# Differential attention: the transposes of a step written in front of the next projection, and the value matmuls written as all high parts, then all low parts

## The chip, the cores and the metric

The kernel runs on one core of one Trainium2 chip. The metric is device time in microseconds (us) of one execution; 1 us is about 0.06% of the whole. Engines are named as in the profile: PE (TensorE matmuls) with PEld (its weight loads), DVE (VectorE), ACT (ScalarE), POOL (GpSimd) and SP (SyncE, which only issues transfers here).

## What is computed

The program is one decoder block: an RMS norm and one wide input projection, two attention mixers side by side, a gated merge, an output projection and a SwiGLU network. The change touches mixer A, differential attention, with 4 heads, blocks of 128 queries and 1024 positions:

```python
def one_block(i):
    s0 = i * DIFF_Q_BLOCK
    qb = lax.dynamic_slice_in_dim(q, s0, DIFF_Q_BLOCK, axis=1)
    s = jnp.einsum('bqhcd,bkhcd->bhcqk', qb, k).astype(jnp.float32) * scale
    qpos = s0 + jnp.arange(DIFF_Q_BLOCK)
    causal = kpos[None, :] <= qpos[:, None]
    p = jax.nn.softmax(jnp.where(causal, s, NEG_INF), axis=-1)
    a = p[:, :, 0] - lam * p[:, :, 1]
    return jnp.einsum('bhqk,bkhe->bqhe', a.astype(v.dtype), v)
```

Each head has two score matrices (c = 0 and 1); the second softmax is subtracted from the first with the weight lam, and the difference multiplies the values.

## The kernel before

Every float32 product is made of fp32r matmuls: an operand is split into a high part (a rounded copy, made by ACT or DVE) and a low part (the rest, made by DVE), and the products high x high, high x low and low x high are added up in PSUM. In the value product the two parts of v lie side by side, so that one matmul of 256 columns (line 497, the **high** value matmul) gives high x (high, low), and one of 128 columns (line 498, the **low** value matmul) adds low x high.

Mixer A is a loop of 32 **steps**, n = 8h + i for head h and query block i (lines 541 to 561). Before the change, iteration n of the loop writes down, in this order: `d_project(n+2)`, the **projection** of a later step, 24 matmuls of 384 columns into PSUM bank b1 (lines 159 to 161), then the rope products (lines 288 to 290) and the split of v (lines 420, 421), which read the bank and free it; `d_transpose(n+1)`, four **query transposes** (lines 436, 437) into bank b0, from where ACT makes qh (line 442), DVE ql (443) and ACT the transposed keys kT (444); `d_scores(n+1)`, the **scores** of a step (lines 461 to 464) and their softmax (minimum on DVE, line 465; exponential on ACT, 466; lines 468 to 471); `d_values(n)`, which for up to four key blocks at a time makes **probability transposes** (line 486), also into bank b0, then ah on ACT (491) and al on DVE (492), and then the value matmuls into bank b2; and one or two **merge units**, each 24 matmuls of 512 columns into bank b3 (`merge_unit`, lines 315 to 338), work of another part of the program that is put here to fill TensorE.

A step has i + 1 key blocks, so for i of 4 and more there are two groups of probability transposes, the first of four blocks, the second of one to four. Both groups and the query transposes share bank b0: each has to wait until ACT and DVE have read the one before.

This written order is not the order of the engines. A scheduler in the tile framework takes it as a priority, plays the program on a model of time and gives each engine a fixed list of instructions; each engine then runs its list in order. So what the change does to an engine's list is seen in the lists themselves, not in the diff.

The projections and merge units are the work that stands on TensorE's list between a transpose and the matmul that needs its result. It is called **cover** below.

Of the kernel before, what the change touches and what calls it, by code (L numbers as in the profile page):

```python
# [94 lines left out]
def hybrid_block(ctx: ExitStack, tc: tile.TileContext, x, positions, attn_norm_g, w_in, diff_lambda,  # L95
# [3 lines left out]
    V, A, G, T = nc.vector, nc.scalar, nc.gpsimd, nc.tensor  # L99
# [137 lines left out]
    def bank(i):  # L237
        return psum.tile([128, 512], F32, name="b%d" % i, bufs=1)

    def tr_tile():  # L240
        banks, n = turn["tr"]
        turn["tr"] = (banks, n + 1)
        return bank(banks[n % len(banks)]).rearrange("p (a b) -> p a b", b=128)
# [58 lines left out]
    def flat(ap):  # L302
        return ap.rearrange("p a b -> p (a b)")
# [9 lines left out]
    st, mg_done = {}, [0]  # L313
# [92 lines left out]
    with pool("da", bufs=2) as da, pool("das", bufs=2) as das:  # L406
# [24 lines left out]
        def d_transpose(n):  # L431
            h, i = divmod(n, NT)
            qd, ks = st.pop(("qk", n))
            tp = tr_tile()
            for c in range(2):
                T.transpose(tp[:, c], flat(qd[:, c]), ident)
                ins = T.transpose(tp[:, 2 + c], flat(ks[:, c]), ident)
            if GT and n >= DH * NT - GT:
                st["last"] = ins
            qh = da.tile([128, 2, 128], R, name="qh")  # L440
            ql = da.tile([128, 2, 128], R, name="ql")
            A.activation(qh, tp[:, 0:2], AF.Copy)
            V.tensor_sub(ql, tp[:, 0:2], qh)
            A.activation(st["kT", h][:, :, i * 128:(i + 1) * 128], tp[:, 2:4], AF.Copy)
            st["q", n] = (qh, ql)
# [28 lines left out]
        def d_values(n):  # L474
            h, i = divmod(n, NT)
            p0 = st.pop(("p", n))
            if i == 0:
                st["y", h] = (da.tile([128, NT, 128], F32, name="yraw"), das.tile([128, NT], F32, name="yss"))
            yraw, yss = st["y", h]
            o = bank(2)[:, :256]  # L480
            parts = []
            for b0 in range(0, i + 1, 4):
                nb = min(4, i + 1 - b0)
                tp = tr_tile()
                for b in range(nb):
                    ins = T.transpose(tp[:, b], p0[:, (b0 + b) * 128:(b0 + b + 1) * 128], ident)
                if b0 == 0 and n >= DH * NT - GLN:
                    st["last"] = ins
                ah = da.tile([128, 4, 128], R, name="ah")
                al = da.tile([128, 4, 128], R, name="al")  # L490
                A.activation(ah[:, :nb], tp[:, :nb], AF.Copy)
                V.tensor_sub(al[:, :nb], tp[:, :nb], ah[:, :nb])
                parts.append((b0, nb, ah, al))
            for b0, nb, ah, al in parts:
                for b in range(nb):
                    vb = flat(st["vv", h][:, b0 + b])
                    T.matmul(o, ah[:, b], vb, start=(b0 + b == 0), stop=False)
                    T.matmul(o[:, 0:128], al[:, b], vb[:, 0:128], start=False, stop=(b0 + b == i))
            ot = da.tile([128, 128], F32, name="ot")
            A.activation(ot, o[:, 128:256], AF.Copy)  # L500
            V.tensor_add(yraw[:, i], o[:, 0:128], ot)
            A.activation(ot, yraw[:, i], AF.Square, accum_out=yss[:, i:i + 1])
# [9 lines left out]
        def compressed_mask():  # L512
            cm32 = da.tile([128, 2, HD], F32, name="cm32", bufs=1)
            for tb in range(0, NT, 2):
                G.memset(cm32, 0.0)
                G.affine_select(cm32, cm32, pattern=[[128, 2], [-16, HD]], compare_op=OP.is_ge, fill=BIG,
                                base=tb * 128 - 31, channel_multiplier=1)
                G.tensor_copy(cmask[:, tb:tb + 2], cm32)
# [13 lines left out]
        N = DH * NT  # L532
# [6 lines left out]
            return first + int(sum(cw[:n + 1]) / sum(cw) * (2 * (2 * KD + NQX) - RES - first) + RES * max(0, n + 1 - N + RLN) / RLN + 1e-6)  # L539

        for n in range(-2, N):
            if n + 2 < N:
                d_project(n + 2)
            if n == -2:
                lam_scalar()
            if n == 10:
                compressed_mask()
            if 0 <= n + 1 < N:
                d_transpose(n + 1)
            if SF and 0 <= n + 1 < N:  # L550
                d_scores(n + 1)
            if n >= 0:
                d_values(n)
            if not SF and 0 <= n + 1 < N:
                d_scores(n + 1)
            while mg_done[0] < mg_target(n):
                merge_unit(mg_done[0])
                mg_done[0] += 1
            if n >= 0:
                if n >= NT and n % NT == 0:  # L560
                    d_norm(n // NT - 1)
# [268 lines left out]
    with lined("na", bufs=2) as na:  # L830
# [137 lines left out]
        for n, u in enumerate(units):  # L968
# [3 lines left out]
            i, hp, br = u  # L972
# [33 lines left out]
    with lined("br") as br, pool("brp", space=PSUM) as bp:  # L1006
# [25 lines left out]
        for n in range(2 * KD):  # L1032
            b, dm = divmod(n, KD)
# [390 lines left out]
    for n in range(NS):  # L1424
        i, p = divmod(n, HF)
# [54 lines left out]
```

## Time and profile before

| | us |
|---|---|
| median of 3 runs (1718.57 to 1719.31) | 1718.66 |
| the profiled execution, its own time | 1721.26 |
| its span in the trace | 1719.3 |
| TensorE busy in the span | 1647.1 |
| mixer A's steps in the trace | about 45 to 485 |

The page of the profile gives busy time per engine and 40 slices over the span. The timeline gives each instruction with its start, its duration and, in square brackets, the idle time before it and who ended it. Matmuls overlap in their records: the duration of one includes a tail of about 0.2 us that the next one hides, so what a matmul costs is read from start to start.

### The profile page before, as it was taken

The numbers are of one execution on the slowest core, as the hardware profiler recorded it, in microseconds if no ns is written. First come the engines' busy times: TensorE is split into PE (matmuls) and PEld (weight loads), VectorE is DVE, ScalarE is ACT, GpSimd is POOL, SyncE is SP. The second block draws the span as 40 slices with busy tenths as digits, with TensorE's granted clock in tenths as the row PEclk, the third lists the DMA queues.
The fourth block names the chain that finished last, engine by engine and source line by source line (L and its number), as shares of the span: only waits on it lengthen the run. The fifth ranks groups of instructions, "written<-read, shape, count | busy, mean of one in ns | idle before, by whom it ended". The sixth has DMA issues, their size and how long they took to land.

```text
span 1719.3 us, 25072 instructions
## 1 busy us (share of the span) xinstructions
PE 1647.1 (96%) x9025; PEld 1423.3 (83%) x9025; DVE 1090.3 (63%) x2156; ACT 775.1 (45%) x1652; POOL 441.5 (26%) x626
## 2 busy tenths in 40 slices
PE   4999999999999999999999997999999999999997
PEld 3988888988889998998878885788888888888886
DVE  8554545546348768888855339565656556686667
ACT  3334333434424247878854234433333333344445
POOL 4532322323222336657625210011100101000000
PEclk8999999999999999999999998999999999999999
DMA  6120211113213000100184421333332332674433
GB/s 209 47 80 25 81 43 44 50 44 95 86 59 99 29 28 15 50 17 17 26 285 159 172 86 50 111 116 117 113 108 92 102 113 97 209 246 120 135 96 140
DMA packets 150635, 163.68 MB, mean 95 GB/s; under 512 B 11616, under 2 KB 114048, under 8 KB 150512
## 3 DMA queue, kind: packets, MB, share of 16 engines
q1 hardware_dynamic: 138272, 124.90, 23.3%
q0 software_dynamic: 9760, 31.94, 4.9%
q10 hardware_dynamic: 2480, 5.25, 1.0%
q8 instruction: 71, 1.16, 0.3%
q14 instruction: 52, 0.43, 0.1%
HBM read 117.76 MB, written 44.30 MB: 94 GB/s over the span
## 4 chain that ended last, share of the span: by engine, by line
PE 82%; DVE 7%; issue 5%; ACT 3%; POOL 2%; DMA 1%; SPq 0%; ACTq 0%; POOLq 0%; DVEq 0%
PE mm L1140 8%; PE mm L1141 8%; PE mm L1142 8%; PE b L159 5%; PE b L160 5%; PE b L161 5%; PE s L874 3%; PE b L927 3%; PE mm L1386 3%; PE mm L1385 3%; PE mm L1387 3%; PE b L938 3%; PE s L159 2%; PE s L161 2%; PE s L160 2%
## 5 line engine op out<-in xcount | busy, mean ns | idle before, releaser
L1133 ACT ACTIVATE oh<-S 128x512 fp32r<-128x512 f32 x88 | 55.7, 633 | 142.2 <-PE mm L1141 140.1
L159 PE MATMUL b<-uh,mg_h 128*128 128x512 f32 x288 | 114.8, 399 | 0.7 <-ACT mg_st L337 0.7
L160 PE MATMUL b<-ul,mg_h 128*128 128x512 f32 x288 | 113.7, 395 | 0.0
L161 PE MATMUL b<-uh,mg_l 128*128 128x512 f32 x288 | 112.9, 392 | 0.0
L874 PE MATMUL s<-kN,qN 128*128 128x320 f32 (+5 forms) x384 | 100.8, 365 | 3.7 <-ACT p L891 2.7
L942 DVE TENSOR_TENSOR pl<-b,ph 128x512 fp32r<-128x512 f32 (+1 forms) x152 | 90.5, 613 | 12.8 <-ACT ph L941 11.8
L941 ACT ACTIVATE ph<-b 128x512 fp32r<-128x512 f32 (+1 forms) x152 | 80.2, 544 | 32.2 <-PE b L938 30.9
L161 PE MATMUL b<-pw_h,ul 128*128 128x384 f32 x256 | 89.1, 348 | 4.9 <-DVE ul L219 4.9
L891 ACT ACTIVATE p<-s,mn 128x640 f32<-128x640 f32 (+7 forms) x128 | 89.2, 703 | 7.7 <-DVE mn L885 2.4
L159 PE MATMUL b<-pw_h,uh 128*128 128x384 f32 x256 | 90.2, 352 | 2.0 <-ACT uh L218 1.4
L160 PE MATMUL b<-pw_l,uh 128*128 128x384 f32 x256 | 88.7, 347 | 3.5 <-DVE pw_l L269 3.5
L1133 ACT ACTIVATE oh<-raw 128x512 fp32r<-128x512 f32 x66 | 41.5, 632 | 108.3 <-PE mm L1141 105.9
L898 POOL TENSOR_TENSOR p<-p,sm 128x640 f32<-128x640 f32 (+3 forms) x64 | 89.1, 1414 | 2.5
L1387 PE MATMUL mm<-oh,ol 128*128 128x512 f32 x218 | 84.8, 389 | 0.0
L1386 PE MATMUL mm<-ol,oh 128*128 128x512 f32 x218 | 84.8, 389 | 0.0
L938 PE MATMUL b<-ident,p 128*128 128x128 f32 x528 | 83.0, 275 | 1.6 <-POOL p L895 1.0
L465 DVE TENSOR_REDUCE mn<-s 128x1 f32<-128x128 f32 (+7 forms) x64 | 46.0, 753 | 53.9 <-PE s L464 53.8
L1134 DVE TENSOR_TENSOR ol<-S,oh 128x512 fp32r<-128x512 f32 x88 | 59.6, 686 | 31.0 <-ACT oh L1133 26.7
L159 PE MATMUL s<-pw_h,uh 128*128 128x256 f32 (+1 forms) x256 | 75.8, 296 | 2.6 <-ACT xs L648 1.6
L927 PE MATMUL b<-ph,vN 128*128 128x256 f32 x264 | 75.1, 302 | 0.0
L160 PE MATMUL s<-pw_l,uh 128*128 128x256 f32 (+1 forms) x256 | 74.3, 290 | 0.0
L161 PE MATMUL s<-pw_h,ul 128*128 128x256 f32 (+1 forms) x256 | 74.0, 289 | 0.0
(451 smaller groups left out, 5146.8 us busy)
## 6 DMA issues: line engine op xcount, KB each, us to landing
raw<-in_w_gate_dram SPq DMA_DIRECT2D x22, 512.0 KB, 5.1
raw<-in_w_up_dram SPq DMA_DIRECT2D x22, 512.0 KB, 4.6
mg_raw<-in_w_in_dram SPq DMA_DIRECT2D x18, 512.0 KB, 4.6
mgd<-mg_st POOLq DMA_DIRECT2D x32, 256.0 KB, 3.7
sg<-mgd SPq DMA_DIRECT2D x16, 512.0 KB, 4.6
pw_raw<-in_w_in_dram SPq DMA_DIRECT2D x24, 256.0 KB, 3.8
b<-in_w_down_dram SPq DMA_DIRECT2D x22, 256.0 KB, 5.9
xt<-in_x_dram SPq DMA_DIRECT2D x8, 512.0 KB, 5.1
```

The costliest lines, as they stand in the source:

```text
L159: T.matmul(ps, ah, bh, start=(i == 0), stop=False)
L160: T.matmul(ps, ah, bl, start=False, stop=False)
L161: last = T.matmul(ps, al, bh, start=False, stop=(i == n - 1))
L874: T.matmul(s_[:, c], qN[:, 2 * hp + es[c * len(es) // 2], i * 128:(i + 1) * 128], kNs[br][:, v, g, c0:c0 + cw], start=(v == 0), stop=(v == 1))
L927: T.matmul(o, lhsT, rhs, start=(done == 0), stop=(done == total - 1))
L938: T.transpose(tp[:, 2 * (b - b0) + e], p[:, e, b * 128:(b + 1) * 128], ident)
L1133: A.activation(wh, src, AF.Copy)
L1140: T.matmul(ps, w[0][:, k], b[0][:, k], start=(first and k == 0), stop=False, **kw)
L1141: T.matmul(ps, w[0][:, k], b[1][:, k], start=False, stop=False, **kw)
L1142: T.matmul(ps, w[1][:, k], b[0][:, k], start=False, stop=(k == 3), **kw)
L1386: T.matmul(ps, ah[:, ts], wl, start=False, stop=False, **kw)
L1387: T.matmul(ps, al[:, ts], wh, start=False, stop=(p == HF - 1), **kw)
```

## The change

Two pieces of mixer A are written in another order. In the loop, `d_transpose(n+1)` stands in front of `d_project(n+2)`. In `d_values`, the loop over the key blocks is split in two: first every high value matmul of the step, then every low one. The matmuls, their shapes and their number stay the same; the low one's moving operand is named in another way but is the same columns. Lines behind the edit are 3 higher in the changed kernel (the low matmul's is 501 instead of 498, yraw's 504 instead of 501).

```diff
@@ -495,7 +495,10 @@
                 for b in range(nb):
                     vb = flat(st["vv", h][:, b0 + b])
                     T.matmul(o, ah[:, b], vb, start=(b0 + b == 0), stop=False)
-                    T.matmul(o[:, 0:128], al[:, b], vb[:, 0:128], start=False, stop=(b0 + b == i))
+            for b0, nb, ah, al in parts:
+                for b in range(nb):
+                    vh = st["vv", h][:, b0 + b, 0]
+                    T.matmul(o[:, 0:128], al[:, b], vh, start=False, stop=(b0 + b == i))
@@ -539,14 +542,14 @@
         for n in range(-2, N):
+            if 0 <= n + 1 < N:
+                d_transpose(n + 1)
             if n + 2 < N:
                 d_project(n + 2)
...
-            if 0 <= n + 1 < N:
-                d_transpose(n + 1)
             if SF and 0 <= n + 1 < N:
```

The engines' lists show what the scheduler makes of it. Up to step 0 nothing moves and behind mixer A next to nothing; SP's list has one load of merge weights six places earlier. Within mixer A the query transposes keep their place behind the last low matmul of a step in both lists; it is the projections and merge units that change places with the rest. Three places are shown; a name like b_3450 is one tile, here one use of a bank.

**Place 1: PE's list, values of step 21 (i = 5), second group.** b_3450 are the step's sums, b_3460 is the second group of probability transposes, b_3964 a projection. Before:

```order
L497 MATMUL b_3450<-vv,ah 128x256
L159 MATMUL b_3964<-pw_h,uh 128x384
L160 MATMUL b_3964<-pw_l,uh 128x384
L161 MATMUL b_3964<-pw_h,ul 128x384
L486 MATMUL b_3460<-ident,p_3291 128x128 x2
L498 MATMUL b_3450<-vv,al 128x128
L497 MATMUL b_3450<-vv,ah 128x256
L498 MATMUL b_3450<-vv,al 128x128
```

In the changed kernel the two transposes into b_3460 stand 20 merge matmuls ahead of these rows (b_4050 is the merge unit's bank):

```order
L159 MATMUL b_4050<-uh,mg_h 128x512
L160 MATMUL b_4050<-ul,mg_h 128x512
L161 MATMUL b_4050<-uh,mg_l 128x512
L497 MATMUL b_3450<-vv,ah 128x256 x2
L501 MATMUL b_3450<-vv,al 128x128 x6
L436 MATMUL b_3511<-ident,qd 128x128
L437 MATMUL b_3511<-ident,ks 128x128
L436 MATMUL b_3511<-ident,qd 128x128
```

Before, the second group is followed at once by the low matmul of an earlier block and then by alternating pairs; now most of a merge unit stands between the transposes of the second group and their high matmuls, and the low matmuls come last.

**Place 2: PE's list, scores of step 9 (head 1, block 1).** b_1696 and b_1695 are the probability transposes and the sums of step 8. Before, the last query transposes of step 9 and what follows them:

```order
L436 MATMUL b_1663<-ident,qd 128x128
L437 MATMUL b_1663<-ident,ks 128x128
L159 MATMUL b_1714<-uh,mg_h 128x512
L160 MATMUL b_1714<-ul,mg_h 128x512
L161 MATMUL b_1714<-uh,mg_l 128x512
```

And, still before, the end of the scores of step 9 and what follows them:

```order
L463 MATMUL s<-causalb,identb 128x128
L464 MATMUL s<-kT,ql 128x256
L486 MATMUL b_1696<-ident,p_1539 128x128
L159 MATMUL b_2151<-pw_h,uh 128x384
L160 MATMUL b_2151<-pw_l,uh 128x384
L161 MATMUL b_2151<-pw_h,ul 128x384
```

In the changed kernel, from the last query transposes of step 9 to the high matmul of step 8:

```order
L436 MATMUL b_1623<-ident,qd 128x128
L437 MATMUL b_1623<-ident,ks 128x128
L461 MATMUL s<-kT,qh 128x256
L463 LDWEIGHTS identb
L463 MATMUL s<-causalb,identb 128x128
L464 MATMUL s<-kT,ql 128x256
L461 MATMUL s<-kT,qh 128x256
L463 LDWEIGHTS identb
L463 MATMUL s<-causalb,identb 128x128
L464 MATMUL s<-kT,ql 128x256
L486 MATMUL b_1696<-ident,p_1539 128x128
L497 MATMUL b_1695<-vv,ah 128x256
```

Before, a whole merge unit stands between the query transposes and the scores, and 22 matmuls of a projection between the probability transpose and its high matmul (the first rows of each are shown); now there is nothing in either gap. Over the whole list, the gap between query transposes and scores is empty in 6 steps before (8 and 27 to 31) and in 8 now (9, 16, 23, 25 and 28 to 31); in 6 more it now holds two merge matmuls (17, 22), three (15), or three matmuls of a projection (24, 26, 27). The gap between a group of probability transposes and its first high matmul held seven matmuls or more before; now it is empty at steps 8, 16 and 24 (one block) and for the first group of step 22 (four blocks), and holds one matmul for the second groups of steps 23 (four blocks) and 28 (one). Two merge units that had two transposes and seven value matmuls between them at step 29 now have the two transposes alone.

**Place 3: DVE's list and PE's, around the scores of step 23 (i = 7).** b_3612 and b_3621 are the first and second group of probability transposes of step 22, which come right behind these scores; b_3611 are its sums. DVE before:

```order
L288 TENSOR_TENSOR t_3989<-b_3964,ropeC 128x256
L289 TENSOR_TENSOR t_3990<-b_3964,ropeS 128x4x32
L290 TENSOR_TENSOR t_3990<-b_3964,ropeS 128x4x32
L421 TENSOR_TENSOR vv<-b_3964,vv 128x128
L465 TENSOR_REDUCE mn<-s 128x1 x2
L492 TENSOR_TENSOR al<-b_3612,ah 128x512
```

DVE now:

```order
L465 TENSOR_REDUCE mn<-s 128x1 x2
L288 TENSOR_TENSOR t_3999<-b_3974,ropeC 128x256
L289 TENSOR_TENSOR t_4000<-b_3974,ropeS 128x4x32
L290 TENSOR_TENSOR t_4000<-b_3974,ropeS 128x4x32
L492 TENSOR_TENSOR al<-b_3612,ah 128x512
L468 RECIPROCAL rc<-sm 128x2
```

PE now, from the end of these scores:

```order
L463 MATMUL s<-causalb,identb 128x128
L464 MATMUL s<-kT,ql 128x512
L486 MATMUL b_3612<-ident,p_3429 128x128 x4
L497 MATMUL b_3611<-vv,ah 128x256 x4
L486 MATMUL b_3621<-ident,p_3429 128x128 x3
L159 MATMUL b_4088<-pw_h,uh 128x384
```

Before, the rope reads and the split of v stand ahead of the two minima (line 465), and on PE a projection separates the first group from the second; now the rope reads stand between the minima and al (line 492), and PE has the second group's transposes four high matmuls behind the first group's.

## Rows read from the trace of the kernel before

**Rows 1.** The page, busy time of TensorE and its share of the span

```profile
PE 1647.1 (96%) x9025; PEld 1423.3 (83%) x9025; DVE 1090.3 (63%) x2156; ACT 775.1 (45%) x1652; POOL 441.5 (26%) x626
```

**Rows 2.** Waits, 40 to 490 us: who waited for whom, total us, times, longest

```profile
PEld b L498 <- DVE al L492: 4.3, 9, 0.7
```

**Rows 3.** Timeline of PE in step 14: start, duration, instruction, idle before, releaser

```profile
265.94 0.38 PE L497 MATMUL b<-vv,ah 128*128 128x256 f32 x1
266.80 0.33 PE L498 MATMUL b<-vv,al 128*128 128x128 f32 x1 [0.48 <-DVE al L492]
266.96 0.33 PE L497 MATMUL b<-vv,ah 128*128 128x256 f32 x1
267.13 0.22 PE L498 MATMUL b<-vv,al 128*128 128x128 f32 x1
267.19 0.33 PE L497 MATMUL b<-vv,ah 128*128 128x256 f32 x1
```

**Rows 4.** Timeline of PE in mixer B: sixteen 64-column matmuls in a row

```profile
670.27 2.06 PE L841 MATMUL s<-kC,qN 128*128 128x64 f32 x16
```

**Rows 5.** Timeline, query transposes to scores with no cover (blocks 3 and 4)

```profile
409.75 0.27 PE L437 MATMUL b<-ident,ks 128*128 128x128 f32 x1
410.48 0.42 DVE L443 TENSOR_TENSOR ql<-b,qh 128x256 fp32r<-128x256 f32 x1 [0.27 <-ACT qh L442]
411.37 0.50 PE L461 MATMUL s<-kT,qh 128*128 128x512 f32 x1 [1.35 <-ACT kT L444]
...
419.48 0.27 PE L437 MATMUL b<-ident,ks 128*128 128x128 f32 x1
420.23 0.73 PE L461 MATMUL s<-kT,qh 128*128 128x512 f32 x2 [0.47 <-ACT qh L442]
```

**Rows 6.** Timeline, probability transposes to ah and al, one block and four

```profile
236.62 0.27 PE L486 MATMUL b<-ident,p 128*128 128x128 f32 x1
237.24 0.29 DVE L492 TENSOR_TENSOR al<-b,ah 128x128 fp32r<-128x128 f32 x1
...
383.73 0.60 PE L486 MATMUL b<-ident,p 128*128 128x128 f32 x4
384.36 0.60 ACT L491 ACTIVATE ah<-b 128x512 fp32r<-128x512 f32 x1 [2.85 <-PE b L486]
```

**Rows 7.** Timeline, scores of 1024 columns: transposes, two minima, al

```profile
364.77 0.60 PE L486 MATMUL b<-ident,p 128*128 128x128 f32 x4
...
364.37 2.36 DVE L465 TENSOR_REDUCE mn<-s 128x1 f32<-128x1024 f32 x2 [4.20 <-PE s L464]
366.64 0.68 DVE L492 TENSOR_TENSOR al<-b,ah 128x512 fp32r<-128x512 f32 x1
```

**Rows 8.** Timeline of PE, two merge units with nothing between them

```profile
492.59 0.50 PE L159 MATMUL b<-uh,mg_h 128*128 128x512 f32 x1 [0.69 <-ACT mg_st L337]
492.93 0.40 PE L160 MATMUL b<-ul,mg_h 128*128 128x512 f32 x1
493.16 0.39 PE L161 MATMUL b<-uh,mg_l 128*128 128x512 f32 x1
```

**Rows 9.** Timeline of PE, a projection that waits for its bank

```profile
157.91 0.41 PE L159 MATMUL b<-pw_h,uh 128*128 128x384 f32 x1 [0.59 <-DVE vv L421]
158.17 0.34 PE L160 MATMUL b<-pw_l,uh 128*128 128x384 f32 x1
158.34 0.34 PE L161 MATMUL b<-pw_h,ul 128*128 128x384 f32 x1
```

**Rows 10.** Stretches: length; busy PE, PEld, DVE, ACT, POOL; PE's clock; DMA

```profile
163.40:166.80 3.40, 1.84 (x15) 1.41 (x13) 1.94 (x6) 1.33 (x5) 1.55 (x4) 1.00 0.00 0
166.80:170.30 3.50, 3.50 (x17) 3.50 (x16) 1.77 (x7) 1.99 (x7) 0.46 (x1) 0.51 0.00 0
...
409.10:412.50 3.40, 2.05 (x15) 1.39 (x14) 1.83 (x6) 1.61 (x6) 2.00 (x5) 1.00 1.11 363
```

**Rows 11.** Groups by shape on DVE, 60 to 490 us: the cast of merge weights

```profile
L326 DVE CAST mg_h<-mg_raw 128x1024 fp32r<-128x1024 f32 x16 | 11.2, 700 | 19.0 <-PE b L160 19.0
```

## The prediction

> **What bounds the kernel now.** The page comes first: TensorE is busy for 96% of the span [rows 1], so it is the bound, and time moves only by what its list waits for or loses. The next view is the table of waits, cut to mixer A: what TensorE waits for there is short. The largest entry is the low value matmuls on al [rows 2]. From the timeline I then read what such a wait costs, always from start to start: in [rows 3] the low matmul starts 0.86 us after the high one where 0.17 is usual, so this wait costs 0.69, though its idle time reads 0.48. Last, I went through the new list of TensorE for the gaps between a transpose and its user, and priced each empty one by a place of the old trace where a like gap was empty.
>
> **The matmuls themselves.** 144 high and 144 low matmuls change order, none is added. An alternating pair costs 0.23 us (266.96 to 267.19 [rows 3]). No row has 128-column value matmuls in a row; the nearest has 64-column ones, of which sixteen take 2.06 us, 0.11 to 0.13 each [rows 4]. The 64-column ones are no cheaper than half a pair, so something other than columns sets the pace, which I take to be the weight load that each matmul has. High ones alone I put at 0.12, low ones alone at 0.11: a pair stays at 0.23, and regrouping costs nothing. The other end is that a low one behind a low one takes 0.06, as the step from a low to a high does (267.13 to 267.19 [rows 3]); then 144 x 0.05 = 7 us would go.
>
> The Trainium skill, page "TensorE: Matmul & The Clock Gate", section "Back-to-back issue gap", gives about 81 ns for each of a stream of 128-column matmuls with weight loads. By it regrouping would bring about 144 x 0.03 = 4 us (an estimate from that page); the 64-column row speaks against so short a pace, and the sum goes by the row.
>
> **What goes.** In the old list the second group of a step has only seven value matmuls between its transposes and the first al, and ten low matmuls wait for al. Nine of those waits are the 4.3 us of [rows 2]; the matmul after each loses another 0.10 (266.80 to 266.96 is 0.16 instead of 0.06 [rows 3]). That is 4.3 + 10 x 0.10 = 5.3 us. The low matmuls now come last, behind four or more others, and al is long done: all of it goes. So does one wait of a projection for its bank, 0.6 us idle, 0.8 with what follows (158.17 comes 0.26 after 157.91, not 0.17) [rows 9], since the list now has other work there. Together 6.1 us.
>
> **What comes: query transposes to scores.** With no cover, the scores of blocks 0 to 3 start 1.62 us after the last query transpose, since their first matmul reads the new kT, which ACT makes after DVE's ql; blocks 4 to 7 start with old keys and need only qh: 0.75 us [rows 5]. Less 0.03 that an unhindered start takes, an empty gap costs **1.59** or **0.72**. A merge matmul covers 0.23 [rows 8], a projection's 0.17 [rows 9]. Before, six steps are empty: 8 and 27 at 1.59, 28 to 31 at 0.72, sum 6.1. Now: 9, 16 and 25 empty, 3 x 1.59 = 4.8; 24, 26 and 27 with three projection matmuls, 3 x (1.59 - 0.52) = 3.2; 23 and 28 to 31 empty, 5 x 0.72 = 3.6; 22 with two merge matmuls, 0.3. At step 17, two merge matmuls, but a cast of merge weights (0.70 [rows 11]) now stands in front of ql on DVE; ql would start 0.73 after the transposes [rows 5], and starts some 0.45 later: 1.59 - 0.46 + 0.45 = 1.6. Step 15, with three, loses 0.2 to the same cast. Sum 13.7, so **+7.6 us**. The bounds: if kT came as early as qh, every gap would cost 0.72 at most and the net be about +2; nothing here speaks for that.
>
> **Probability transposes to high matmuls.** For one block al starts, so ah is done, 0.62 us after the transpose; for four, ah is done at 384.96, 0.90 after the last of them (which starts some 0.33 behind the first) [rows 6]. Steps 8, 16 and 24 lose 0.58 each, step 8 a further 0.2 since its low matmul follows at once: 1.9. Step 22's first group, four blocks and no cover: 0.9. The second groups of 23 and 28 have one matmul as cover: 0.7 and 0.35. And at step 22 the second group's transposes need bank b0, which al's read frees. Before, al ends there at 367.32, 2.2 us after the last of the four transposes, because two minima stand ahead of it on DVE [rows 7]; now the three rope reads stand there too (none over the 0.42 that a read of 256 columns takes in [rows 5]; I take 0.8 for all). TensorE is back at 1.4 with four high matmuls done, and waits until 3.0: 1.6, with 0.8 and 2.1 as ends. Sum **+5.5 us**.
>
> **Merge units and projections.** Step 29's two units now have two transposes (0.2) between them. With nothing between, the wait is 0.69 [rows 8]: +0.6, allowing for what the idle time leaves out. The last projection follows the one before it with only the scores of step 26 and two transposes between, and its bank is freed by a read that stands behind two minima on DVE. [rows 9] shows one such wait; I take 1.2 for it and its neighbour, with 0 and 2.5 as ends. Sum **+1.8 us**. Merge weights, POOL's query and key tiles and SP's moved load are ready a step or more ahead in both lists: nothing.
>
> **The clock.** In one stretch of mixer A TensorE's granted clock is 0.51, that is 1.2 GHz, for 3.5 us (so some 1.7 us are lost), after waits for al and for kT that left it busy for 1.84 of 3.40 us; around 410, with the one wait for kT alone, it stays at 2.4 GHz [rows 10]. Those first waits change or go; but the new list has four places where waits crowd as closely: steps 8/9 (1.59, 0.58, 0.2), 16/17, 22/23 (0.7, 0.9, 1.6) and 24/25 (0.7, 1.59, 0.58). I take two half-speed stretches for the one: **+1.7 us**, with -1.7 and +5 as ends.
>
> The same page of the Trainium skill, section "Why this matters for your kernels", puts a fall of the clock down to a long idle gap between bursts of matmuls. By it none of these gaps would cost clock, and the sum would be 1.7 us lower; [rows 10] shows a fall after a sum of short ones, so the row decides.
>
> **Sum.** 7.6 + 5.5 + 1.8 - 6.1 + 1.7 = **+10.5 us**. The profiled execution took 1721.26 us, 2.6 over the median of the three runs (0.15%); the difference is worked out inside that execution and put on the median, 1718.66 + 10.5 = **1729.2 us**. Why a list with the same work comes out worse: each step has one projection and at most one or two merge units as cover. Before, they lay in the two long gaps of a step; now a third gap, in front of the second group's high matmuls, takes one, and from step 9 on gaps are left empty. What is late next is ACT and DVE's chain of qh, ql and kT.
>
> **The rivals.** (1) Faster: the waits for al go, and TensorE's new gaps cost as little as before, because ACT and DVE, less pressed by a waiting TensorE, answer at once. With 6.1 and the half-speed stretch gone, 1718.7 - 7.8 = 1711. It decides the sign if the new waits stay under 4.3 us together. Against it: the prices in [rows 5, 6] are taken where ACT and DVE were free. Chance 0.09. (2) About the same: the new waits come to half of my sum, since some run at the same time as others, which gives 14.9 / 2 - 6.1 = +1.4, 1720. Chance 0.11. (3) Low matmuls in a row run at 0.06: 1729.2 - 7 = 1722; the page's 81 ns above gives 1725. [rows 4] speaks against the first. Chance 0.06, mostly on the line between same and slower. (4) Much slower: the clock falls at all four crowded places and the bank waits are at their upper ends: +5 and +2, 1736. For it: three of the four have more waiting in a row than the stretch that fell. Chance 0.14. The forecast has 0.60, and its own bounds reach from 1724 to 1734.
>
> **How the numbers follow.** The range 1720 to 1737 takes in the forecast, rival 4, most of 3 and half of 2. The measurement can tell about 0.2% from no change, 3.4 us: faster means under 1715.2, slower over 1722.1. Faster has rival 1, 0.09; same has rival 2 and most of 3, 0.15; slower the rest, 0.76.
>
> **What would show it.** In the profile after: no wait of low matmuls on al worth naming; scores waiting for kT or qh some fourteen times, 0.7 or 1.6 us each, at steps 9, 16, 17 and from 22 on; high matmuls waiting for ah at steps 8, 16, 22, 23 and 24; one wait of transposes for al at step 22; pairs of value matmuls at 0.23 us when grouped; more than one stretch at half clock before 490 us; and everything behind mixer A shifted as a whole. I am wrong if the scores' waits stay near 6 us together, or if grouped low matmuls start 0.06 us apart.

## The result and the profile after

The changed kernel takes **1741.41 us**, median of four runs (1737.33 to 1743.8); the kernel before, beside it, 1718.99. The ratio is 1.0128 with an interval of 1.0114 to 1.0142: slower by 22.4 us. The direction was forecast, the size was not: the forecast was +10.5, and the time lies 4 us above the range.

In the profiled execution (1742.57 us) all of the loss is made in mixer A. From the first query transpose to the last matmul of the last merge unit it takes 461.4 us instead of 438.9, +22.5; the rest of the program takes 1279.5 instead of 1280.4. The page has TensorE busy for 10.8 us more than [rows 1], though it has not one matmul more:

```profile
PE 1657.9 (95%) x9025; PEld 1430.4 (82%) x9025; DVE 1085.8 (62%) x2156; ACT 774.0 (44%) x1652; POOL 443.5 (25%) x626
```

The table of waits of TensorE, cut to 60 to 520 us (who waited for whom, idle us in total, times, longest):

```profile
PE s L461 <- ACT kT L444: 7.8, 7, 1.3
PE b L159 <- DVE vv L421: 3.5, 3, 1.5
PE s L461 <- ACT qh L442: 2.5, 5, 0.5
PE b L497 <- ACT ah L491: 2.3, 5, 0.7
PE b L486 <- DVE al L492: 1.3, 1, 1.3
PE b L159 <- ACT mg_st L337: 1.2, 2, 0.7
PE b L501 <- DVE al L492: 0.9, 1, 0.9
```

The same table of the kernel before, cut to 60 to 500 us:

```profile
PE s L461 <- ACT kT L444: 2.7, 2, 1.3
PE b L498 <- DVE al L492: 2.2, 6, 0.5
PE s L461 <- ACT qh L442: 1.9, 4, 0.5
...
PE b L159 <- DVE vv L421: 0.6, 1, 0.6
```

The low matmuls' six waits for al are one ([rows 2] counts nine, those of the weight loads). In their place scores wait for kT and qh twelve times instead of six, high matmuls for ah five times, and projections for vv, which is the last read of their bank, three times instead of once. The timeline of TensorE at the first crowded place, steps 8 and 9:

```profile
192.12 0.64 PE L497 MATMUL b<-vv,ah 128*128 128x256 f32 x4
192.59 1.01 PE L501 MATMUL b<-vv,al 128*128 128x128 f32 x8
193.43 0.29 PE L436 MATMUL b<-ident,qd 128*128 128x128 f32 x1
...
193.78 0.27 PE L437 MATMUL b<-ident,ks 128*128 128x128 f32 x1
195.40 0.38 PE L461 MATMUL s<-kT,qh 128*128 128x256 f32 x1 [1.35 <-ACT kT L444]
...
196.27 0.42 PE L486 MATMUL b<-ident,p 128*128 128x128 f32 x1
197.05 0.58 PE L497 MATMUL b<-vv,ah 128*128 128x256 f32 x1 [0.37 <-ACT ah L491]
198.55 0.48 PE L501 MATMUL b<-vv,al 128*128 128x128 f32 x1 [0.92 <-DVE al L492]
...
201.14 0.69 PE L159 MATMUL b<-pw_h,uh 128*128 128x384 f32 x1 [1.24 <-DVE vv L421]
201.63 0.53 PE L160 MATMUL b<-pw_l,uh 128*128 128x384 f32 x1
201.95 0.53 PE L161 MATMUL b<-pw_h,ul 128*128 128x384 f32 x1
```

Query transpose to scores is 1.62 us, as in [rows 5]. Four high matmuls in a row take 0.47 (192.12 to 192.59), eight low ones 0.84 (to 193.43): 0.12 and 0.105 each, so a grouped pair is 0.22 us, as forecast. But four waits follow each other between 193.9 and 201.1, and among them the matmuls get slow: a projection's is 0.32 us from start to start (201.63 to 201.95) instead of 0.17 [rows 9]. Stretches of the same place, with the columns of [rows 10]:

```profile
192.80:196.20 3.40, 2.05 (x18) 1.73 (x17) 1.92 (x5) 1.45 (x6) 3.25 (x3) 1.00 0.00 0
196.20:199.60 3.40, 2.12 (x9) 1.36 (x7) 3.30 (x17) 1.57 (x6) 1.18 (x4) 0.50 0.83 231
199.60:203.00 3.40, 2.16 (x8) 1.86 (x7) 2.75 (x14) 1.51 (x6) 1.93 (x5) 0.50 0.01 2
203.00:206.40 3.40, 3.40 (x12) 3.40 (x11) 1.36 (x6) 0.00 (x0) 0.56 (x1) 0.50 0.18 76
```

TensorE runs at 1.2 GHz from 196.2, right behind the first of the four waits, to 206.4, and the last third of that is full of matmuls. The records of the granted clock have four more such stretches in mixer A, of 3.4 us each, from 295.2, 315.6, 397.6 and 418.0: in all **23.9 us at half speed**, where before there were 3.4.

**A sum for each kernel.** For each pair of matmuls that follow each other I took from the trace the time from start to start, less what such a pair takes unhindered. What is over by more than 0.15 us is a wait. In a half-speed stretch the excess is put down to the clock, up to the matmul's own time. What is left after waits and clock is 424.9 us before and 426.0 in the changed kernel, and between 424.9 and 426.2 in every run below (434.5 where matmuls were added), so the two accounts explain nearly all differences in mixer A. The rest of the program takes 1275 to 1284 us from one profile to another, with half-speed stretches of its own that go with no edit; for small effects mixer A is the better measure.

| kernel | time, us | ratio to before, interval | mixer A | waits | of them scores | clock | at half speed |
|---|---|---|---|---|---|---|---|
| before | 1718.99 | | 438.9 | 12.4 | 5.6 | 1.6 | 3.4 |
| changed | 1741.41 | 1.0128, 1.0114 to 1.0142 | 461.4 | 25.8 | 13.2 | 9.6 | 23.9 |
| after_again | 1739.54 | 1.0121, 1.0107 to 1.0134 | 459.5 | 26.5 | 13.2 | 6.9 | 17.1 |
| norm_later | 1739.63 | 1.0133, 1.0115 to 1.0150 | 459.0 | 26.1 | 13.2 | 6.7 | 17.1 |
| order_only | 1746.15 | 1.0168, 1.0154 to 1.0182 | 463.7 | 28.8 | 12.4 | 9.0 | 23.9 |
| regroup_only | 1723.14 | 1.0032, 1.0021 to 1.0043 | 442.0 | 16.7 | 5.7 | 0 | 0 |
| gaps_apart | 1725.53 | 1.0043, 1.0029 to 1.0056 | 447.9 | 18.6 | 15.2 | 3.3 | 6.8 |
| fill | 1737.06 | 1.0109, 1.0093 to 1.0124 | 454.3 | 16.7 | 5.9 | 3.1 | 6.8 |
| norm_fill | 1737.57 | 1.0116, 1.0099 to 1.0133 | 453.7 | 16.6 | 5.9 | 2.7 | 6.8 |
| norm_held | 1735.95 | 1.0102, 1.0087 to 1.0118 | 453.9 | 22.5 | 13.5 | 5.5 | 13.7 |
| held_fill | 1729.95 | 1.0074, 1.0057 to 1.0091 | 451.0 | 14.9 | 4.9 | 1.6 | 3.4 |
| parts | 1718.31 | 1.0002, 0.9993 to 1.0010 | 438.4 | 11.2 | 5.7 | 1.6 | 3.4 |
| split | 1715.73 | 0.9987, 0.9976 to 0.9998 | 436.0 | 10.9 | 1.5 | 0 | 0 |
| both | 1715.75 | 0.9985, 0.9976 to 0.9993 | 435.9 | 9.1 | 1.5 | 1.6 | 3.4 |

The times are medians; from mixer A on, the columns are us of the profiled execution. Each of these rows is one profile. One and the same list (changed, after_again, norm_later) gave 23.9, 17.1 and 17.1 us at half speed, so one stretch of 3.4 us more or less between two kernels shows nothing by itself.

### The profile page after: what moved, and what is told of

Its sections match the earlier page's. It is cut to its first block, busy times and chain, and to the rows that moved or that the text cites. A ratio compares the mean times of both kernels' runs of the same rounds, so it can differ in the third digit from the quotient of the medians.

```text
span 1740.9 us, 25094 instructions
## 1 busy us (share of the span) xinstructions
PE 1657.9 (95%) x9025; PEld 1430.4 (82%) x9025; DVE 1085.8 (62%) x2156; ACT 774.0 (44%) x1652; POOL 443.5 (25%) x626
## 4 chain that ended last, share of the span: by engine, by line
PE 84%; DVE 7%; issue 3%; ACT 3%; DMA 1%; POOL 1%; SPq 0%; ACTq 0%; POOLq 0%; DVEq 0%
PE mm L1143 8%; PE mm L1144 8%; PE mm L1145 8%; PE b L159 6%; PE b L160 6%; PE b L161 6%; PE s L877 3%; PE b L930 3%; PE mm L1388 3%; PE mm L1389 3%; PE mm L1390 3%; PE b L941 3%; PE s L159 2%; PE s L160 2%; PE s L161 2%
## 5 line engine op out<-in xcount | busy, mean ns | idle before, releaser
L930 PE MATMUL b<-pl,vN 128*128 128x256 f32 x264 | 72.3, 296 | 1.5 <-DVE pl L945 1.5
```

The lines of the kernel that those rows point to most:

```text
L930: T.matmul(o, lhsT, rhs, start=(done == 0), stop=(done == total - 1))
```

## The experiments

**Which of the two edits.** Each was made alone, on the kernel before. order_only has the loop edit and leaves the value matmuls alternating; regroup_only has the other.

```diff
 order_only
+            if 0 <= n + 1 < N:
+                d_transpose(n + 1)
             if n + 2 < N:
                 d_project(n + 2)
...
-            if 0 <= n + 1 < N:
-                d_transpose(n + 1)
 regroup_only
-                    T.matmul(o[:, 0:128], al[:, b], vb[:, 0:128], start=False, stop=(b0 + b == i))
+            for b0, nb, ah, al in parts:
+                for b in range(nb):
+                    vh = st["vv", h][:, b0 + b, 0]
+                    T.matmul(o[:, 0:128], al[:, b], vh, start=False, stop=(b0 + b == i))
```

> Only the loop order is changed, the value matmuls alternate as before. Theory (the loss is made by the loop order: it takes the cover away at heads' ends, and the crowded waits bring the clock down): by the list, empty gaps from query transposes to scores cost 13.3 us against 6.1, from probability transposes to high matmuls 3.4 against 0.1, and the half-speed stretches in mixer A add up to 14 to 24 us against 3.4; 1732 to 1741 us. Rival (the regrouping of the value matmuls makes the loss): 1716 to 1722 us, half speed 3 to 7 us.

> Only the value matmuls are regrouped, the loop order is as before. Theory: the list keeps its rhythm of one merge unit in front of the scores and one projection in front of the values; the waits for al go (-5.0 us), thirteen second groups have their high matmuls right behind their transposes and wait for ah, by the list 8.3 us; waits lie apart, so half speed stays at 3 to 7 us in mixer A; 1719 to 1724 us. Rival (short matmuls in groups bring the clock down): half speed over 14 us, 1727 us or more.

order_only takes 1746.15 us, more than both edits together and 5 us over what was expected; its half speed is 23.9 us. regroup_only takes 1723.14, as expected, and its clock does not fall in mixer A at all. So the loop order makes the loss, and short matmuls in groups do not bring the clock down. What was not expected is how the two go together: alone they cost 28.3 and 5.3 us, together 22.4. The waits tell why. order_only:

```profile
PE s L461 <- ACT kT L444: 7.6, 6, 1.3
PE b L498 <- DVE al L492: 3.7, 3, 1.7
PE b L486 <- DVE al L492: 3.3, 2, 1.7
PE b L159 <- DVE vv L421: 2.9, 2, 1.6
```

and regroup_only:

```profile
PE b L497 <- ACT ah L491: 5.8, 12, 0.7
PE s L461 <- ACT kT L444: 2.7, 2, 1.3
```

With the old loop order, regrouping turns the waits for al into twelve waits for ah, since the second group's high matmuls now stand right behind its transposes. With the new loop order, it takes away long waits for al (the second and third row of order_only) which that order makes.

**Is it the crowding that costs clock?** gaps_apart is the kernel before with one number changed. It makes as many gaps in front of the scores as the changed kernel has, but a step apart and with all high matmuls covered.

```diff
-GLN = 6
+GLN = 24
```

> The kernel before, with one number changed: merge units are held back until the probability transposes of a step from step 8 on, not only from step 26 on. The list then has as many empty gaps between query transposes and scores as the changed kernel (14.3 us by the prices of the prediction; 13.0 in the changed kernel, 6.1 before), but they lie a step apart, and no high matmul is without cover. Theory (the clock falls where several kinds of wait crowd within a few us, not where one long one stands alone): half speed in mixer A 0 to 10 us against 23.9 in the changed kernel, 1722 to 1728 us. Rival (a long wait for kT alone brings the clock down): 17 us or more at half speed, 1730 us or more.

fill is the changed kernel with matmuls that do nothing, in the gaps in front of the scores:

```diff
+FILL = {9: 6, 16: 6, 17: 4, 23: 2, 24: 3, 25: 6, 26: 3, 27: 3}
                 sc.append(s_)
+                if c == 0 and n in FILL:
+                    with tc.issue_after(st["t", n].ins):
+                        for k in range(FILL[n]):
+                            T.matmul(s_[:, :512], uh[:, 0, 0:128], uh[:, 0, 0:512], start=True, stop=True)
```

> The changed kernel with 33 matmuls of 512 columns added, whose results are overwritten and not used, in the gaps between query transposes and scores of steps 9, 16, 17 and 23 to 27; they keep TensorE busy there and end before the scores can start, so no wait gets shorter or longer. Theory (empty waits that crowd bring TensorE to half speed, and this is the part of the loss that was forecast too small): half speed in mixer A under 14 us against 23.8 in the changed kernel, 1732 to 1738 us. Rival (the clock falls for another reason): 20 us or more at half speed, 1740 to 1744 us.

gaps_apart came out as the theory said: the scores wait 15.2 us, 2 more than in the changed kernel (2.3 of that is one wait for ql at step 28), and 6.8 us are at half speed. Of these, 3.4 are the stretch at 166.8 that the kernel before has too; the other 3.4, at 429.7, come behind that wait for ql, which has a wait of 0.6 for qh right in front of it. Its two long waits for kT at steps 8 and 9 are 12 us apart (the second, as at step 9 of the changed kernel, is 1.35 idle), and the clock holds around the second; nor does it fall at steps 17 or 25:

```profile
177.00:180.40 3.40, 2.05 (x13) 1.72 (x13) 3.10 (x15) 2.17 (x9) 2.02 (x5) 1.00 0.00 0
284.00:287.40 3.40, 2.05 (x16) 1.69 (x15) 2.50 (x12) 1.82 (x8) 2.01 (x5) 1.00 0.35 108
392.00:395.40 3.40, 2.05 (x15) 1.60 (x14) 2.82 (x13) 2.11 (x8) 2.01 (x5) 1.00 0.28 84
```

This does not say that a wait for kT alone never brings the clock down. In the changed kernel the stretch at 295.2 stands behind the wait of step 16 alone; for 14 us before it TensorE has no other wait over 0.15 us:

```profile
294.65 0.33 PE L461 MATMUL s<-kT,qh 128*128 128x128 f32 x1 [1.35 <-ACT kT L444]
```

```profile
295.20:298.60 3.40, 3.40 (x15) 3.29 (x15) 2.06 (x7) 1.91 (x7) 0.40 (x1) 0.50 0.00 0
```

In the two later profiles of the same list the clock holds at this place. In the fourteen profiles together, thirteen waits of 1.35 us for kT have no other wait over 0.15 us in the 7 us before them and the 4 us behind them, and this fall is the only one that follows such a wait. And at steps 8/9 the clock fell, in the first profile and in that of norm_held (196.2 and 196.1), behind the wait for kT, before the next wait had come. So what goes with the crowding is how often the clock falls and how long it stays down; one wait can be enough. The sum of waits does not explain it either: regroup_only waits 16.7 us, as long as fill, mostly in pieces that lie apart, and has no half speed in mixer A.

fill has 6.8 us at half speed, not 23.9, and it falls later at the first place: at full clock where the changed kernel was slow, and slow only once two more waits (al, 1.31 idle, and vv, 1.21) had followed each other.

```profile
192.80:196.20 3.40, 3.40 (x22) 2.55 (x21) 2.20 (x5) 1.33 (x5) 3.38 (x4) 1.00 0.04 2
196.20:199.60 3.40, 1.19 (x7) 0.74 (x6) 3.30 (x19) 2.07 (x9) 1.46 (x5) 1.00 0.83 229
201.20:204.60 3.40, 3.40 (x13) 3.40 (x12) 2.23 (x9) 0.00 (x0) 0.56 (x1) 0.50 0.00 0
```

Mixer A gets 5 to 8 us shorter (453.7 and 454.3 against 459.0 to 461.4 in the three profiles of the changed kernel) by matmuls that compute nothing. At steps 16, 17 and 25 the fall is gone; the two that stay, at 201.2 and 392.3, are where waits that fill leaves alone still crowd. Against the expectation two waits of projections went as well: at step 16 from 1.77 to 0.36 us, and the one of 1.0 at the last projection. In the account the added matmuls cost 8.3 to 8.5 us and take away 9.1 to 9.8 of waits, which nearly cancel; the clock gives back 3.6 to 6.5. As a whole, fill's interval overlaps that of the changed kernel; in its one profile the rest of the program took 2.5 us more. The evidence is in mixer A and its clock.

**What is the same from run to run.** after_again is the changed kernel once more.

> The changed kernel once more, for a second profile of the same lists. Theory (the waits are a matter of the lists, the clock is what differs from run to run): waits over 0.15 us in mixer A again 26 to 28 us, half speed 14 to 28 us, times 1737 to 1744 us that go with the granted clock. Rival (the waits differ from run to run): their sum differs by over 2 us at like clock.

The waits come out the same (26.5 against 25.8 us), half speed is 17.1 instead of 23.9: the clock is what differs. A third profile of the same list of TensorE, norm_later, agrees (26.1 and 17.1). In all three the clock falls at steps 8/9, 16/17, 22/23 and 24/25, which are the four places that the prediction named; the stretch at 295.2, behind a lone wait, is in the first alone. The four runs of the result show it too: at a mean granted clock of 0.984, 0.981, 0.979 and 0.978 they took 1737.3, 1740.3, 1742.6 and 1743.8 us.

**Why do projections and one low matmul wait so long?** These waits (1.61 us in front of the projection at 201.14, 1.77 in front of another at 314.6, 1.26 for al at 198.55) were hardly in the forecast. DVE's timeline at steps 8 and 9 shows what it does instead (lines 168 to 181 are the norm of the head that step 7 has finished):

```profile
194.51 0.43 DVE L443 TENSOR_TENSOR ql<-b,qh 128x256 fp32r<-128x256 f32 x1 [0.27 <-ACT qh L442]
194.85 0.45 DVE L168 TENSOR_SCALAR sub_a<-yss 128x8 f32<-128x8 f32 x1
195.34 0.47 DVE L170 TENSOR_SCALAR sub_r<-sub_a 128x8 int32<-128x8 int32 x1
195.84 0.88 DVE L178 TENSOR_TENSOR sub_t<-sub_r 128x8 f32<-128x8 f32 x1
...
197.40 0.41 DVE L465 TENSOR_REDUCE mn<-s 128x1 f32<-128x256 f32 x1
...
198.22 0.28 DVE L492 TENSOR_TENSOR al<-b,ah 128x128 fp32r<-128x128 f32 x1
...
200.35 0.42 DVE L443 TENSOR_TENSOR ql<-b,qh 128x256 fp32r<-128x256 f32 x1 [0.55 <-ACT qh L442]
...
200.81 0.28 DVE L421 TENSOR_TENSOR vv<-b,vv 128x128 fp32r<-128x128 f32 x1
```

Two causes stand here. The scores' minima (line 465) come late behind the norm, and al behind them. And vv, which frees the projection's bank, stands behind ql of step 10, which waits for qh, which waits for the query transposes of step 10: the loop order itself has put the transposes of a step ahead of the reads of a projection. To test the first cause I wrote the norm later; norm_fill has fill's edit besides.

```diff
-                if n >= NT and n % NT == 0:
+                if n >= NT and n % NT == 3:
                     d_norm(n // NT - 1)
```

> The changed kernel with one condition altered: the norm of a finished head, a chain of small instructions on DVE (lines 168 to 181 and 512), is written three steps later, at block 3 of the next head instead of block 0. TensorE's list keeps its order. Theory (the wait of step 8's low matmul for al, 1.26 us, and the two waits of projections for their bank at the heads' ends, 1.61 and 1.77 us, are long because that chain stands in front of al and of the reads of the bank on DVE): these three fall to under 1.8 us together, and with them some half speed at 196 and 315 us; 1734 to 1739 us. Rival (the reads of the bank are late for their own length): the three stay over 4 us, 1739 to 1743 us.

> Both the later norm and the 33 added matmuls of the run fill. Theory (two separate causes): waits over 0.15 us in mixer A 13 to 15 us against 16.8 in fill and 26.9 in the changed kernel, half speed in mixer A 0 to 7 us; 1732 to 1736 us, 1 to 4 us under fill. Rival (the later norm only moves its waits): 1736 us or more.

This tested nothing: the three waits stayed (1.45, 1.61 and 1.78 us), because the norm stands at the same places of DVE's list as before; why the scheduler left it there is not shown. The runs serve as second profiles of the changed kernel and of fill, and say the same (16.6 us of waits and 6.8 at half speed for norm_fill, there all at steps 8/9). The next pair holds the norm back by data; held_fill adds fill's edit.

```diff
+                if n >= NT and n % NT == 3:
+                    yraw_, yss_ = st["y", n // NT - 1]
+                    z = das.tile([128, NT], F32, name="z", bufs=1)
+                    G.tensor_scalar(z, st["qk", n + 2][0][:, 0, 0, 0:NT], 0.0, None, op0=OP.mult)
+                    G.tensor_add(z, z, yss_)
+                    st["y", n // NT - 1] = (yraw_, z)
+                    d_norm(n // NT - 1)
```

> The changed kernel with the norm of a finished head held back by data: its input takes a zero, made by POOL from a tile of three steps later, so that in DVE's list it stands at steps 11, 19 and 27 instead of 9, 17 and 25 (in the run norm_later it had not moved in that list at all). The list of TensorE is the same up to step 16; from there two high matmuls get cover (1.2 us). Theory (the norm in front of al and of the reads of the bank makes step 8's al wait of 1.3 to 1.5 us and the projections' waits of 1.6 and 1.8 us at steps 8 and 16): the three fall to under 1.8 us together, mixer A's waits over 0.15 us from 27 to 22 to 24; with less crowding also less half speed, 1731 to 1737 us. Rival (they are late for the minima and the reads alone): the three stay over 3.5 us, 1737 to 1743 us.

> The held norm of norm_held and the 33 added matmuls of fill together. Theory (two causes side by side): waits over 0.15 us in mixer A 12 to 15 us against 16.8 in fill, half speed 0 to 7 us, 1731 to 1735 us. Rival: as fill, 1736 us or more.

norm_held takes 1735.95 us, inside what the theory gave, held_fill 1729.95, 1 us below it. Not all of the 6 us between them is shown to come from the added matmuls: in the profiles mixer A differs by 2.9, and the rest of the program, where none of them stands, by 5.6. At steps 8 and 9, where TensorE's list is unchanged, norm_held shows:

```profile
197.22 0.58 PE L497 MATMUL b<-vv,ah 128*128 128x256 f32 x1 [0.37 <-ACT ah L491]
197.60 0.42 PE L501 MATMUL b<-vv,al 128*128 128x128 f32 x1
...
200.03 0.69 PE L159 MATMUL b<-pw_h,uh 128*128 128x384 f32 x1 [1.13 <-DVE vv L421]
```

The wait for al is gone: that was the norm. The projection's stays at 1.50 us, so it is not the norm's. order_only has it too (1.7 us at 201.3) and regroup_only has none at these steps, so it comes with the loop order; that ql in front of vv is the link is read from DVE's list, and no run takes it away. At step 16 the wait of 1.77 is 0.48 now, but there the list has also moved by one high matmul, so that not all of it is the norm's. The three together are 2.0 us against 4.6, a little over the 1.8 that I had set. The half-speed stretch at step 16/17 is gone with them, and held_fill is left with one, of 3.4 us, at steps 22/23.

**A version that keeps the good half.** parts keeps the old loop order, lets the second group's transposes go first, and then writes each group's high matmuls and its low ones:

```diff
+                if i >= 4:
+                    gate.enter_context(tc.issue_after(ins.ins))
+                for b0, nb, ah, al in parts:
+                    for b in range(nb):
+                        T.matmul(o, ah[:, b], flat(st["vv", h][:, b0 + b]), start=(b0 + b == 0), stop=False)
+                    for b in range(nb):
+                        T.matmul(o[:, 0:128], al[:, b], st["vv", h][:, b0 + b, 0], start=False, stop=(b0 + b == i))
```

> The loop order as before; the transposes of the second group ahead of all value matmuls of the step, then for each group its high ones, then its low ones. Theory (a low matmul's wait for al is 0.5 us of TensorE each, and is gone where eight value matmuls of the first group cover the second group's ah and al): 1712 to 1716 us, waits for al under 1.5 us together against 5.0. Rival (a pair costs more when grouped, or the second group's transposes wait for their bank instead): 1718 us or more.

It takes 1718.31 us, no change, where 1712 to 1716 was expected. The waits of low matmuls fall from 4.9 to 2.6 us, but in head 0, where the list is less even, a projection's wait for its bank grows from 0.8 to 2.2. So the rival of a moved wait was right in one place. split leaves the values alone and cuts late merge units in two:

```diff
+        cut = 2 if "tl" in st else 0
+        for lo, hi, key in ((0, cut, "tl"), (cut, KD, "last")):
+            with ExitStack() as gate:
+                if key in st:
+                    gate.enter_context(tc.issue_after(st[key].ins))
+                for k in range(lo, hi):
...
+            if n >= 27:
+                st["tl"] = ins
```

> The kernel before; from step 27 on the first six matmuls of a merge unit are let go right behind the query transposes, the other eighteen behind the probability transposes as before. Theory (an empty gap costs its full price and six merge matmuls, 1.4 us, are enough to cover it): the gaps of steps 27 to 31 fall from 4.1 us to under 0.6, 1712.5 to 1715.5 us. Rival (the gap is hidden or moves to the merge unit's bank or to the high matmuls): 1717 us or more.

> The kernel before with the merge units split from step 27 on, and with the value matmuls in groups, each group's high ones and then its low ones, behind the second group's transposes, from step 8 on alone; steps 0 to 7 alternate as before. Theory (the two gains lie at different places and add): gaps -3.6 us, waits for al from step 8 on from 3.6 us to 1.3; 1710 to 1714 us. Rival (grouping has a price of its own that cancelled the gain in all steps): 1714 to 1717 us.

split takes 1715.73 us and the run both (split, and parts from step 8 on) 1715.75, ratios 0.9987 and 0.9985 with intervals below 1 (0.9998 and 0.9993 at the upper end): they beat the kernel before, by 2.5 us, and with it the changed one. Six matmuls cover a gap: the scores wait 1.5 us instead of 5.6. The time is 0.2 us over the range that was expected of split, and the run both lies in its rival's range: the first piece of a merge unit now stands close behind the unit before it and waits for its bank; in the run both:

```profile
418.12 0.79 PE L340 MATMUL b<-uh,mg_h 128*128 128x512 f32 x1 [1.67 <-ACT mg_st L345]
```

That grouping brings anything beyond the split is not shown: the two times are equal within their intervals. The waits are 1.8 us less, but the profile of the run both has a half-speed stretch of 3.4 us that split's has not.

## Why the prediction was wrong in size

By its own steps, from the profile of the result:

| step | forecast | measured |
|---|---|---|
| waits for al that go | -5.3 | -4.9 |
| query transposes to scores | +7.6 | 13.2 - 5.6 = +7.6 |
| probability transposes to high matmuls, al at step 8, bank b0 | +5.5 | 3.4 + 1.3 + 1.5 = +6.2 |
| projections' bank (0.8 goes, 1.2 comes) | +0.4 | 4.7 - 0.8 = +3.9 |
| merge units | +0.6 | +0.7 |
| clock | +1.7 | +8.0 (5.3 and 5.1 in the two later profiles) |
| what neither account holds | | +1.1 |
| sum | +10.5 | +22.6 (by mixer A 22.5) |

**What held.** The price list of [rows 5] and [rows 6], put on the gaps of the list, gave the net of the scores' waits to a tenth, at the fourteen steps named. In part that is luck: an empty gap costs 0.1 less than its price (1.5 us for kT, 0.6 for qh), before as well as now, and step 15 costs 0.8 instead of 0.2. The bank wait at step 22 was forecast at 1.6 and is 1.5, the waits around the last projection at 1.2 and are 1.1. Grouped pairs run at 0.22 us, so rival 3 falls; low matmuls in a row start 0.105 us apart. The Trainium skill's figure for 128 columns (page "TensorE: Matmul & The Clock Gate", section "Back-to-back issue gap", 81 ns) is not reached. Rivals 1 and 2 fall with the waits, which neither shrank nor ran side by side.

**The step that failed most** is the clock: "I take two half-speed stretches for the one". The four crowded places were named rightly and the clock fell at every one of them, in each of three profiles; at the first for 6.8 to 10.2 us, not 3.4; the fifth stretch, behind a lone wait, came in one of the three. Against +1.7 that makes +8.0 in the first profile, +5.3 and +5.1 in the later ones. This was rival 4's mechanism, with a chance of 0.14; its +5 is what the later profiles show and is short for the first. (Its time of 1736 counts 1.7 us of clock twice: with +5 in place of +1.7, and +2, it is 1734.5.) The argument ("three of the four have more waiting in a row than the stretch that fell") was in the text, and pointed to four; the sum took two. The rule of the Trainium skill that the prediction weighed there (page "TensorE: Matmul & The Clock Gate", section "Why this matters for your kernels", a fall after a long idle gap) would have given no loss at all, which by the prediction's own lower end (-1.7) is 3.4 us off the sum, not 1.7; in the changed kernel no idle gap in front of a fall is longer than 1.5 us, and the measurement decides.

**The second** is the projections' bank, +3.5 us beyond the forecast. I priced one place, the last projection, from TensorE's side. I did not go through DVE's list at the heads' ends, where the norm and the next ql stand in front of vv. The same omission made al at step 8 cost 1.3 us instead of 0.2. DVE's new list, which was at hand, has both. In the two later profiles, where the clock is 3.6 and 3.4 us over its forecast, the two steps weigh about the same.

The clock's 6.3 us, the projections' 3.5 and the unexplained 1.1 are nine tenths of the 12.1 that were missing.

## What to carry to other kernels

When an edit moves filler work, count the gaps that it leaves empty and price each by a row: here single gaps came out about 0.1 us from their price, but for one that was 0.6 off. Then look at how the gaps lie: a wait that stands alone mostly costs its own time (one fall of the clock behind thirteen such waits), while waits of several kinds behind one another cost a slower clock on top, for longer than they last, at all four places in three profiles; so forecast that at every crowded place and not at half of them. And follow the in-order lists of the engines that answer, here DVE, for small work that stands in front of the instruction waited for; six merge matmuls covered a gap of 1.6 us in split, where a whole unit has twenty-four.

## What was not expected of the hardware

Instructions of the norm on 8 columns take 0.15 to 0.17 us where they do not meet a long one of POOL, and much longer where they do. At step 16, DVE:

```profile
311.34 0.28 DVE L290 TENSOR_TENSOR t<-b,ropeS 128x128 f32<-128x128 f32 x1
311.54 1.83 DVE L170 TENSOR_SCALAR sub_r<-sub_a 128x8 int32<-128x8 int32 x1
313.40 0.47 DVE L178 TENSOR_TENSOR sub_t<-sub_r 128x8 f32<-128x8 f32 x1
```

and POOL:

```profile
310.98 2.36 POOL L327 TENSOR_TENSOR mg_l<-mg_raw,mg_h 128x1024 fp32r<-128x1024 f32 x1
313.27 0.56 POOL L338 DMA_DIRECT2D mgd<-mg_st  x1
```

The instruction of 8 columns ends at 313.37, when POOL's at 310.98 ends (313.34); the one behind it ends with POOL's next. It repeats in the other two profiles of this list (1.83 us each). The rope reads at 311.34 and before it, which take one operand from PSUM, run at their usual time beside the same POOL instruction. This is how the projection at step 16 came to wait 1.77 us. The Trainium skill, page "SBUF — State Buffer", section "SBUF: two separate sides", states that VectorE and GpSimd share a pair of ports, used by GpSimd's instructions and by those of VectorE that run in a two-port mode or have two inputs in SBUF (these against GpSimd instructions that read SBUF), and that whoever starts first holds it for its whole instruction. The rows agree; that the instruction of line 170, which has one input, ran in such a mode is not shown by any row. The runs fill and norm_fill bear out that POOL is the cause: there its instruction of line 327 starts later, line 170 takes 0.16 us, the projection waits 0.36, and it is line 179 that meets POOL. In fill, DVE and POOL:

```profile
310.03 2.15 DVE L179 TENSOR_TENSOR sub_t<-sub_t,sub_a 128x8 f32<-128x8 f32 x1
```

```profile
309.75 2.39 POOL L327 TENSOR_TENSOR mg_l<-mg_raw,mg_h 128x1024 fp32r<-128x1024 f32 x1
```

The one ends at 312.18, the other at 312.14.
